# A diffusion step's expert lookup: more steps of the choice a chunk, and half of a product in three rounded parts

## The chip, the cores and the metric

One core of a Trainium2 chip runs the whole program. The metric is the time of one execution on the device in microseconds (us). Of the kernel before three runs are known: 5380.45, 5382.38 and 5386.86 us, median 5382.38.

## What is computed

One inference step of a backbone with two streams, 128 context tokens and 512 latent tokens of width 2048. The first half of the layer (a token mixer of three branches) isn't touched by the change. The second half, which is, looks up experts by product keys:

```python
v1, i1 = lax.top_k(s1, 16); v2, i2 = lax.top_k(s2, 16)     # 8 heads, 128 keys each
cand = (v1[..., :, None] + v2[..., None, :]).reshape(tok, 8, 256)
top, sel = lax.top_k(cand, 16)                             # 128 experts a token
g = jax.nn.softmax(top, axis=-1)
act = jnp.einsum("cd,ckd->ck", xc, u_tab[ic])              # first table, 16384 x 2048
w = gc * jax.nn.gelu(act)
out = jnp.einsum("ck,ckd->cd", w, v_tab[ic])               # second table, 16384 x 2048
```

Both tables are float32.

## The kernel before, in words

The 640 tokens are five blocks of 128. For each block `choose` (L1034) finds the experts that any token of the block uses: it writes a dense matrix of weights `G_d` (16384 experts by 128 tokens, mostly zeros) to memory in four stores of 2 MB from the tile `Gs`, and a list `L_d` of the used experts. `experts` (L1371) then goes over that list in chunks of 256 rows: it gathers 256 rows of the first table, multiplies them with the block's tokens, weighs the result, and adds the product with 256 rows of the second table to an accumulator in PSUM. The first 24 chunks of a block (K0) always run; each later one stands in an `If` on the length of the list. In this run there are 134 chunks in all.

One chunk is a generator, `chunk` (L1262), with nine yields. In the order of the program:

- `gather_u`: an indirect DMA, issued by POOL, for 128 rows of the first table into `ur` for the next chunk.
- `turn(g)` for g = 0 to 7 (L1229): four transposes of 128 columns into PSUM (`tb`), a copy to a rounded float32 half `wh` on ACT (L1237), the rest `wl` by a subtract on VectorE (DVE, L1238).
- `up(g)` (L1240): six products of 256 columns, three for each of two slices: rounded x rounded, rounded x rest, rest x rounded. A product of two rounded operands is one pass of TensorE; one of full float32 operands is two instructions of two passes each.
- the last `up` of a chunk, `up(7)`, stands in the next chunk and ends with the gelu on ACT (L1247). Then `weigh` (L1249) transposes the result and multiplies it with the weights `gr` on VectorE into `w`.
- `gather_g` (two gathers from `G_d` into `gr`), `entries` (two gathers of list entries `ix` for three chunks on), the second `gather_u`. All are issued by POOL.
- `down(u)` for u = 0 to 7 (L1256): one full float32 product of 512 columns each, of the half j = u // 4 of the weights with a quarter of `vr[j]`, the tile of 128 rows of the second table. In the steps g = 2 to 7 it stands between `turn(g)` and `up(g - 1)`; the last two stand at the end. These are the products of the chunk before.
- `gather_v(0)` refills `vr[0]` behind `down(3)`, `gather_v(1)` refills `vr[1]` at the chunk's end.

Each engine works off its instructions in this order. `pin` (L1357) ties every instruction of an engine to the one before it, so nothing is moved. POOL issues all the indirect gathers, one after the other.

The choice for the next block is itself a generator, advanced between the yields of the chunks: `more` takes a step at every odd yield of the first 24 chunks of a block (four a chunk), `fin`, the finishing of the last block, at every even one. What is left of the choice behind chunk 23 runs without a chunk beside it (`for _ in more: pass`). Its steps: 33 up to the one-hot tiles, then a loop of 34 rounds at L1102 in which VectorE writes one-hot tiles `oh` and `dd`, TensorE multiplies them (L1116), ACT copies the result to `Gs` (L1107), and after every eight results `Gs` is stored; four steps behind each store count the used experts (L1132); then 14 steps that write the list and gather its first entries. `Gs` is one buffer, so the next copy into it waits for the store.

Of the kernel before, what the change touches and what calls it, by code (L numbers as in the profile page):

```python
# [7 lines left out]
F32 = mybir.dt.float32  # L8
F32R = mybir.dt.float32r
# [142 lines left out]
class Kern:  # L152
# [881 lines left out]
    def choose(self, b, S=None):  # L1034
# [50 lines left out]
        g = I12[:, 2].rearrange("p (h k) -> p h k", k=16)  # L1085
# [10 lines left out]
        p = ps.tile([128, 3, 128], F32, name="g", tag="m", bufs=1)  # L1096
# [5 lines left out]
        for n in range(34):  # L1102
            if full is not None:
                n1, p = full
# [7 lines left out]
            if ready is not None:  # L1112
                n1, oh, dd = ready
                p = ps.tile([128, 4, 128], F32, name="g", tag="m", bufs=1)
# [4 lines left out]
            if n < 32:  # L1119
                oh = T.tile([128, 4, 128], F32, name="oh", tag="oa", bufs=2)  # L1120
                dd = T.tile([128, 4, 128], F32, name="dd", tag="od", bufs=2)
                for j in range(4):
                    k1, k2, w = (it[:, i, n * 4 + j:n * 4 + j + 1] for i in range(3))
# [6 lines left out]
            if n % 8 == 1 and n > 1:  # L1130
                for q in range(4):
                    v.tensor_reduce(cnt[:, n // 8 - 1, q * 32:q * 32 + 32], st[:, q * 32:q * 32 + 32], axis=AX.X,  # L1132
                                    op=ALU.add)
                    yield

        f = T.tile([128, 128], F32, name="f", tag="f", bufs=1)
        v.tensor_reduce(f, cnt.rearrange("p q i -> p i q"), axis=AX.X, op=ALU.add)
        v.tensor_scalar(f, f, 0.0, None, op0=ALU.is_gt)
# [6 lines left out]
        for r in range(16):  # L1145
            s = slice(r * 8, r * 8 + 8)
# [26 lines left out]
        p = ps.tile([128, 128], F32, name="g", tag="m", bufs=1)  # L1173
# [4 lines left out]
        p = ps.tile([128, 128], F32, name="g", tag="m", bufs=1)  # L1178
# [4 lines left out]
        p = ps.tile([128, 128], F32, name="g", tag="m", bufs=1)  # L1183
# [56 lines left out]
    def up(self, g, x):  # L1240
# [5 lines left out]
        if g == 7:  # L1246
            self.nc.scalar.activation(self.t, self.a, AF.Gelu_apprx_tanh)  # L1247

    def weigh(self):  # L1249

        p = self.bank()[:, :256].rearrange("p (j t) -> p j t", j=2)
        for j in range(2):
            self.nc.tensor.transpose(p[:, j], self.t[:, j * 128:j * 128 + 128], self.ident)  # L1253
        self.nc.vector.tensor_mul(self.w, p, self.gr)  # L1254

    def down(self, u, first):  # L1256

        j, d = divmod(u, 4)
        self.nc.tensor.matmul(self.acc[:, d], self.w[:, j], self.vr[j][:, d * 512:d * 512 + 512],  # L1259
                              start=first and j == 0, stop=j == 1, skip_group_check=True)  # L1260

    def chunk(self, i, c, pending, rows=None):  # L1262


        nc, b = self.nc, self.order[i]
        self.nbank = 1
        x = self.xs[i % 2]
        rows = rows or self.ur[c % 2]
        if c + 1 < NCH:
            self.gather_u(b, c + 1, 0)  # L1270
        self.turn(0, rows)
        if pending is not None:
            first, before = pending
            self.up(7, before)
        self.turn(1, rows)
        yield
        if pending is not None:
            self.weigh()
        self.gather_g(b, c)
        if c + 3 < NCH:  # L1280
            self.entries(b, c + 3)
        self.up(0, x)
        yield
        if c + 1 < NCH:
            self.gather_u(b, c + 1, 1)
        for g in range(2, 8):
            self.turn(g, rows)
            if pending is not None:
                self.down(g - 2, first)
                if g - 2 == 3:  # L1290
                    self.gather_v(b, c, 0)
            self.up(g - 1, x)
            yield
        if pending is not None:
            self.down(6, first)
            self.down(7, first)
        else:
            self.gather_v(b, c, 0)
        self.gather_v(b, c, 1)
        yield  # L1300
# [70 lines left out]
    def experts(self):  # L1371
        nc, tc = self.nc, self.tc
        E = self.E = self.pool("experts")
        one = lambda shape, name, dt=F32: E.tile(shape, dt, name=name)
        self.vr = [one([128, D], "vr%d" % j) for j in range(2)]
        self.y = one([128, D], "fy")
        self.t = one([128, CH], "t")
        self.gr, self.w = one([128, 2, 128], "gr"), one([128, 2, 128], "w")
        self.ur = [[one([128, D], "ur%d%d" % (c, j)) for j in range(2)] for c in range(2)]
        hb = self.H[GB]  # L1380
        self.xs = [[t[:, j] for t in hb] for j in range(2)]
        first = [one([128, D], "uf%d" % j) for j in range(2)]
        pieces = [[t[:, k * 512:k * 512 + 512]
                   for t in [self.wp.tile([128, 1024], F32R, name=n, tag=n, bufs=self.hl_bufs) for _ in range(3)]
                   for k in range(2)] for n in ("wh", "wl")]
        self.uh, self.ul = ([t.rearrange("p (k e) -> p k e", k=2) for t in p[:4]] for p in pieces)
        self.rr, self.nrow = [t.bitcast(F32) for p in pieces for t in p[4:]], 0
        self.fx = [self.wp.tile([128, 1024], F32, name="wr", tag="wr", bufs=self.raw_bufs) for _ in range(2)]
        ps = self.pool("ps5", space=PSUM)
        self.acc = ps.tile([128, 4, 512], F32, name="acc")  # L1390
        self.tb = [ps.tile([128, 512], F32, name="tb%d" % j) for j in range(2)]
        self.a = ps.tile([128, CH], F32, name="a")
        pending, rows, fin = None, None, iter(())
        mark = self.pin()
        self.load_x(0)
        for j in range(2):
            self.gather_u(self.order[0], 0, j)
        for i, b in enumerate(self.order):
            more = self.choose(self.order[i + 1]) if i < 4 else iter(())
            for c in range(K0):  # L1400
                if c == 0 and i:
                    fin = self.finish(i - 1)
                    next(fin)
                for n, _ in enumerate(self.chunk(i, c, pending, rows)):
                    next(more if n % 2 else fin if c else iter(()), None)
                if c == 0:
                    next(fin, None)
                rows, pending = None, (c == 0, self.xs[i % 2])
                if c == 0 and i < 4:
                    self.load_x(i + 1)  # L1410
            for _ in more:
                pass
            if i < 4:
                rows = first
                for j in range(2):
                    self.gather_u(self.order[i + 1], 0, j, first[j])
            n = nc.values_load(self.lists[b]["count"][0:1, 2:3].bitcast(I32), min_val=0, max_val=NE,
                               skip_runtime_bounds_check_because="it counts the ones among 16384 flags")
            self.pin(mark)
            pending = False, self.xs[i % 2]  # L1420
            with contextlib.ExitStack() as st:
                for c in range(K0, NCH):
                    st.enter_context(tc.If(n > c * CH, name="more%d_%d" % (i, c)))
                    mark = self.pin()
                    for _ in self.chunk(i, c, pending):
                        pass
                    self.pin(mark)
            mark = self.pin()
        self.nbank = 1
        self.up(7, pending[1])  # L1430
        self.weigh()
        for u in range(8):
            self.down(u, False)
        for _ in self.finish(4):
            pass
        self.pin(mark)
        self.close(ps, E)
# [95 lines left out]
```

## Time and profile before

| what | value |
|---|---|
| median of three runs | 5382.38 us |
| profiled execution | 5390.09 us |
| its span, first to last instruction | 5388.3 us |
| mean granted TensorE clock | 0.950 |
| TensorE busy (PE) | 4825.3 us, 90% |
| VectorE busy (DVE) | 2880.9 us, 53% |
| ScalarE busy (ACT) | 1604.0 us, 30% |
| GpSimd busy (POOL) | 1604.3 us, 30% |

The profile names engines PE, PEld (TensorE's weight loads, which overlap PE), DVE, ACT, POOL and SP. Matmuls are pipelined, so the time of one includes the way through the array; how long each really occupies the engine is the distance between two starts. The issuing of a DMA isn't counted as busy, except POOL's indirect ones. L12 is line 12 of the kernel.

### The profile page before, as it was taken

To read this page: it belongs to the slowest core of one execution; us is meant where nothing else is said; L and a number is where in the kernel's file an instruction comes from. 1 tells how busy PE (TensorE), PEld (TensorE's weight loads), DVE (VectorE), ACT (ScalarE), POOL (GpSimd) and SP (SyncE) were. 2 spreads that over 40 slices of the span, in tenths; PEclk is the share of its full clock that TensorE was granted. 3 is DMA by queue.
4 is the path that set the end of the run, shared out by engine and by line. 5 is a ranking of instruction groups with operands and counts; after the bars stand their busy time and mean duration, and the time that the engine had idled before them with its cause. 6 is when DMAs were issued, how large, how long until landed. Compare 5 with 4: busy or idle time off the path is not lost.

```text
span 5388.3 us, 74433 instructions
## 1 busy us (share of the span) xinstructions
PE 4825.3 (90%) x29015; PEld 4006.4 (74%) x29015; DVE 2880.9 (53%) x6240; ACT 1604.0 (30%) x2561; POOL 1604.3 (30%) x1628
## 2 busy tenths in 40 slices
PE   8999889999999979968999689877998699969997
PEld 3799879999999958758677567655776567746775
DVE  6783683566435553860754475456554564444333
ACT  3324324333132224232233123222332132212222
POOL 2000592000000016434443234323443343324443
PEclk9999999999999989989999799989998899979999
DMA  6544346555234466544677576756776677757665
GB/s 241 195 170 143 123 144 214 182 174 173 94 129 150 142 215 216 139 160 159 241 251 237 171 266 242 245 176 230 262 252 220 205 257 233 238 168 275 256 256 211
DMA packets 576710, 1084.99 MB, mean 201 GB/s; under 512 B 375643, under 2 KB 388955, under 8 KB 501819
## 3 DMA queue, kind: packets, MB, share of 16 engines
q0 software_dynamic: 97712, 596.41, 30.4%
q1 hardware_dynamic: 460394, 429.32, 27.0%
q10 hardware_dynamic: 18208, 54.08, 2.6%
q8 instruction: 239, 3.92, 0.3%
q14 instruction: 157, 1.28, 0.1%
HBM read 967.53 MB, written 112.13 MB: 200 GB/s over the span
## 4 chain that ended last, share of the span: by engine, by line
PE 29%; DMA 9%; DVE 6%; issue 5%; POOL 3%; ACT 2%; another core or an unknown queue 0%; POOLq 0%; DVEq 0%; SPq 0%; ACTq 0%
PE acc L1259 12%; PE a L1245 8%; DMA G_d<-Gs 6%; PE tb L1236 6%; PE g L1116 3%; DVE wl L1238 2%; ACT wh L1237 1%; DMA ix<-L_d,si 1%; POOL ix L1201 1%; POOL gr L1201 1%; PE tb L1253 1%; POOL ur L1201 1%; ACT Gs L1107 1%; DMA ur<-in_pu,ix 0%; DVE f L1149 0%
## 5 line engine op out<-in xcount | busy, mean ns | idle before, releaser
L1238 DVE TENSOR_TENSOR wl<-tb,wh 128x512 fp32r<-128x512 f32 x1072 | 737.6, 690 | 1387.8 <-ACT wh L1237 965.2
L1237 ACT CAST wh<-tb 128x512 fp32r<-128x512 f32 x1072 | 627.1, 586 | 1763.2 <-PE tb L1236 1517.8
L1259 PE MATMUL acc<-vr,w 128*128 128x512 f32 x2144 | 1094.3, 603 | 22.9 <-DVE w L1254 21.3
L1245 PE MATMUL a<-wh,hh 128*128 128x256 f32 x2144 | 957.6, 447 | 25.2 <-issue 18.3
L1236 PE MATMUL tb<-cst,ur 128*128 128x128 f32 x4160 | 645.2, 278 | 32.1 <-DMA ur<-in_pu,ix 30.9
L193 ACT CAST wh<-wr 128x1024 fp32r<-128x1024 f32 x339 | 355.6, 1049 | 977.4 <-PE a L630 364.6
L1245 PE MATMUL a<-wl,hh 128*128 128x256 f32 x2144 | 614.0, 286 | 20.5 <-DVE wl L1238 17.1
L1245 PE MATMUL a<-wh,hl 128*128 128x256 f32 x2144 | 609.8, 284 | 0.0
L1245 PEld LDWEIGHTS a<-wh,hh 128*128 128x128 f32 x2144 | 414.9, 193 | 229.5 <-issue 218.2
L1236 PEld LDWEIGHTS tb<-cst,ur 128*128 128x128 f32 x4160 | 491.5, 143 | 121.7 <-issue 83.2
L1245 PEld LDWEIGHTS a<-wl,hh 128*128 128x128 f32 x2144 | 415.6, 194 | 221.4 <-issue 168.2
L1201 POOL DMA_INDIRECT vr<-in_pv,ix x268 | 253.8, 947 | 1066.7 <-PE acc L1259 1037.2
L630 PE MATMUL a<-h,wl 128*128 128x320 f32 x2368 | 548.4, 311 | 18.4 <-DVE wl L194 18.4
L194 DVE TENSOR_TENSOR wl<-wr,wh 128x1024 fp32r<-128x1024 f32 x281 | 343.8, 1225 | 379.5 <-ACT wh L193 368.0
L630 PE MATMUL a<-h,wh 128*128 128x320 f32 x2368 | 546.7, 311 | 0.0
L630 PE MATMUL a<-l,wh 128*128 128x320 f32 x2368 | 543.7, 310 | 0.0
L630 PEld LDWEIGHTS a<-h,wl 128*128 128x128 f32 x2368 | 398.9, 189 | 20.7 <-DVE wl L194 20.0
L630 PEld LDWEIGHTS a<-h,wh 128*128 128x128 f32 x2368 | 403.4, 189 | 12.1
L1245 PEld LDWEIGHTS a<-wh,hl 128*128 128x128 f32 x2144 | 412.4, 192 | 0.0
L1259 PEld LDWEIGHTS acc<-vr,w 128*128 128x128 f32 x2144 | 341.4, 194 | 94.5 <-issue 68.8
L630 PEld LDWEIGHTS a<-l,wh 128*128 128x128 f32 x2368 | 398.7, 189 | 0.8
L1201 POOL DMA_INDIRECT ix<-L_d,si x298 | 290.3, 974 | 308.0 <-DVE si L1189 212.0
(396 smaller groups left out, 7489.0 us busy)
## 6 DMA issues: line engine op xcount, KB each, us to landing
wr<-in_wmod SPq DMA_DIRECT2D x152, 512.0 KB
wr<-in_win SPq DMA_DIRECT2D x83, 512.0 KB
G_d<-Gs SPq DMA_DIRECT2D x20, 2048.0 KB
wrx<-in_win SPq DMA_DIRECT2D x69, 512.0 KB
wrx<-in_wmod SPq DMA_DIRECT2D x40, 512.0 KB
wr<-in_wo SPq DMA_DIRECT2D x36, 512.0 KB
wr<-in_wq SPq DMA_DIRECT2D x32, 512.0 KB
wrx<-in_wq SPq DMA_DIRECT2D x32, 512.0 KB
```

Source lines behind the costliest of these rows:

```text
L193: nc.scalar.copy(h, raw)
L194: (eng or nc.vector).tensor_sub(l, raw, h.bitcast(F32))
L630: nc.tensor.matmul(a, w, x[:, kt, c0:c0 + n], start=kt == 0 and i == 0, stop=kt == nk - 1 and i == 2)
L1107: nc.scalar.copy(st[:, :, n1 % 8 * 4:n1 % 8 * 4 + 4], p.rearrange("j t i -> j i t"))
L1116: nc.tensor.matmul(p[:, j], oh[:, j], dd[:, j], start=True, stop=True)
L1201: self.nc.gpsimd.indirect_dma_start(out=out, out_offset=None, in_=table, in_offset=bass.IndirectOffsetOnAxis(ap=idx, axis=0))
L1236: nc.tensor.transpose(p[:, k, j * 128:j * 128 + 128], rows[j][:, kt * 128:(kt + 1) * 128], self.ident)
L1237: nc.scalar.copy(self.uh[g % 4], p)
L1238: nc.vector.tensor_sub(self.ul[g % 4], p, self.uh[g % 4].bitcast(F32))
L1245: self.nc.tensor.matmul(self.a, a[:, kt], w[:, k], start=kt + n == 0, stop=kt == 15 and n == 2)
L1253: self.nc.tensor.transpose(p[:, j], self.t[:, j * 128:j * 128 + 128], self.ident)
L1259: self.nc.tensor.matmul(self.acc[:, d], self.w[:, j], self.vr[j][:, d * 512:d * 512 + 512], start=first and j == 0, stop=j == 1, skip_grou ...
```

## The change

The choice advances at every yield, nine steps a chunk, and twenty steps that do nothing follow the four counting steps behind each of the first three stores. `fin` takes the odd yields. The half `vr[0]` of the second table's rows is split by quarters: ACT copies a quarter to a rounded tile `vh`, POOL subtracts it from the row to give the rest `vl`. The weights' first half is split too (`Wh` on ACT, `Wl` on VectorE). `down` takes three products of rounded operands for that half, and the full product for the other. `gather_v(0)` moves from behind `down(3)` to before `down(2)`. `vh` and `vl` lie in a part of older tiles that is free then.

```diff
+                for _ in range(20 if n < 32 else 0):
+                    yield
...
+    def split_v(self, d):
+
+        s = slice(d * 512, d * 512 + 512)
+        self.nc.scalar.copy(self.vh[:, s], self.vr[0][:, s])
+        self.nc.gpsimd.tensor_sub(self.vl[:, s], self.vr[0][:, s], self.vh[:, s].bitcast(F32))
...
         self.nc.vector.tensor_mul(self.w, p, self.gr)
+        self.nc.scalar.copy(self.Wh, self.w[:, 0])
+        self.nc.vector.tensor_sub(self.Wl, self.w[:, 0], self.Wh.bitcast(F32))
...
         j, d = divmod(u, 4)
-        self.nc.tensor.matmul(self.acc[:, d], self.w[:, j], self.vr[j][:, d * 512:d * 512 + 512],
-                              start=first and j == 0, stop=j == 1, skip_group_check=True)
+        s = slice(d * 512, d * 512 + 512)
+        for n, (w, x) in enumerate(((self.w[:, 1], self.vr[1][:, s]),) if j else
+                                   ((self.Wh, self.vh[:, s]), (self.Wh, self.vl[:, s]), (self.Wl, self.vh[:, s]))):
+            self.nc.tensor.matmul(self.acc[:, d], w, x, start=first and j == n == 0, stop=j == 1,
+                                  skip_group_check=True)
...
             first, before = pending
+            self.split_v(0)
             self.up(7, before)
         self.turn(1, rows)
+        if pending is not None:
+            self.split_v(1)
         yield
...
             self.turn(g, rows)
             if pending is not None:
+                if g < 4:
+                    self.split_v(g)
+                if g == 4:
+                    self.gather_v(b, c, 0)
                 self.down(g - 2, first)
-                if g - 2 == 3:
-                    self.gather_v(b, c, 0)
             self.up(g - 1, x)
...
                 for n, _ in enumerate(self.chunk(i, c, pending, rows)):
-                    next(more if n % 2 else fin if c else iter(()), None)
+                    next(more, None)
+                    if c and n % 2:
+                        next(fin, None)
```

Behind the last chunk of all, four `split_v` stand ahead of `weigh`.

## Rows read from the trace of the kernel before

**Rows 1.** The page: busy time by engine, and one of the costliest groups.

```profile
PE 4825.3 (90%) x29015; PEld 4006.4 (74%) x29015; DVE 2880.9 (53%) x6240; ACT 1604.0 (30%) x2561; POOL 1604.3 (30%) x1628
...
L1116 PE MATMUL g<-dd,oh 128*128 128x128 f32 x1280 | 208.5, 313 | 108.5 <-ACT Gs L1107 99.8 <-DVE dd L1125 8.6
```

**Rows 2.** Line 1247, the gelu: duration in ns; whole run, then 2970 to 3210.

```profile
L1247 ACT ACTIVATE t<-a x134: 383/383/384, 2582.7 to 5351.4; 128x256 f32<-128x256 f32 x134
...
L1247 ACT ACTIVATE t<-a x9: 383/383/384, 2975.5 to 3204.7; 128x256 f32<-128x256 f32 x9
```

**Rows 3.** Windows, one chunk: length, busy us (instructions) of PE, PEld, DVE, ACT, POOL; clock.

```profile
5143.68:5160.69 17.01, 16.66 (x100) 12.39 (x98) 5.86 (x9) 5.07 (x9) 7.61 (x8) 1.00 0.70 258
```

**Rows 4.** Timeline of TensorE in that chunk: start, us, instructions merged.

```profile
5150.95 0.60 PE L1236 MATMUL tb<-cst,ur 128*128 128x128 f32 x4
5151.38 1.02 PE L1259 MATMUL acc<-vr,w 128*128 128x512 f32 x2
5151.84 0.69 PE L1245 MATMUL a<-wh,hh 128*128 128x256 f32 x1
...
5152.96 0.60 PE L1236 MATMUL tb<-cst,ur 128*128 128x128 f32 x4
...
5158.98 1.88 PE L1259 MATMUL acc<-vr,w 128*128 128x512 f32 x4
```

**Rows 5.** Timeline of POOL in that chunk; in brackets the idle time before.

```profile
5144.12 0.94 POOL L1201 DMA_INDIRECT vr<-in_pv,ix  x1 [5.38 <-PE acc L1259]
...
5148.69 0.96 POOL L1201 DMA_INDIRECT gr<-G_d,ix  x1 [0.30 <-issue]
5149.95 0.95 POOL L1201 DMA_INDIRECT ix<-L_d,si  x1 [0.30 <-issue]
...
5154.84 0.95 POOL L1201 DMA_INDIRECT vr<-in_pv,ix  x1 [1.42 <-PE acc L1259]
5161.12 0.94 POOL L1201 DMA_INDIRECT vr<-in_pv,ix  x1 [5.34 <-PE acc L1259]
```

**Rows 6.** Waits of POOL over the run: us in total, times, longest.

```profile
POOL vr L1201 <- PE acc L1259: 1037.2, 246, 11.6
```

**Rows 7.** The chain that ended last, at the first block's end: start, us, what.

```profile
2990.12 30.22 DMA G_d<-Gs
...
3040.31 4.61 DVE cnt L1132 x4
...
3064.01 0.95 POOL ix L1201
```

**Rows 8.** Timeline of TensorE in an earlier stage: products of rounded operands, 512 columns.

```profile
1900.51 0.39 PE L957 MATMUL a<-wh,hh 128*128 128x512 f32 x1
1900.74 0.40 PE L957 MATMUL a<-wl,hh 128*128 128x512 f32 x1
```

**Rows 9.** Line 301 on POOL: least, median and most ns of one.

```profile
L301 POOL TENSOR_TENSOR x<-x,xp x16: 1265/1293/2284, 1904.9 to 2163.2; 128x512 f32<-128x512 f32 x16
```

**Rows 10.** Windows around stops of TensorE; the sum is over seven stretches behind stops.

```profile
2917.82:2923.11 5.29, 0.01 (x1) 0.01 (x1) 0.72 (x4) 0.58 (x1) 1.95 (x2) 0.71 0.93 326
2923.11:2926.88 3.77, 3.77 (x15) 3.25 (x15) 0.19 (x1) 0.58 (x1) 0.00 (x0) 0.50 0.26 104
...
3497.74:3503.73 5.99, 5.99 (x22) 4.96 (x23) 0.69 (x1) 0.58 (x1) 0.00 (x0) 0.50 0.02 8
...
sum 30.49, PE 30.48 PEld 26.02 DVE 7.09 ACT 3.58 POOL 2.68; mean PE 4.35 PEld 3.72 DVE 1.01 ACT 0.51 POOL 0.38
```

**Rows 11.** Timelines of POOL and VectorE side by side, in two earlier stretches.

```profile
1989.93 2.41 POOL L194 TENSOR_TENSOR wl<-wr,wh 128x1024 fp32r<-128x1024 f32 x1 [42.76 <-ACT wh L193]
...
1990.20 0.69 DVE L965 TENSOR_TENSOR gy<-a,r 128x512 f32<-128x512 f32 x1 [1.91 <-PE a L957]
...
2163.18 2.27 POOL L301 TENSOR_TENSOR x<-x,xp 128x512 f32<-128x512 f32 x1
...
2158.64 5.66 DVE L1076 TENSOR_TENSOR oh<-oa,cst 128x1024 f32<-128x1024 f32 x2
```

More of the change, by code (lines that the diff above doesn't have):

```diff
@@ L1381, in experts @@
         self.xs = [[t[:, j] for t in hb] for j in range(2)]
+        self.vh, self.vl = (t[:, 2].rearrange("p k t -> p (k t)") for t in hb)
+        self.Wh, self.Wl = (one([128, 128], n, F32R) for n in ("Wh", "Wl"))
         first = [one([128, D], "uf%d" % j) for j in range(2)]
@@ L1430, in experts @@
         self.up(7, pending[1])
+        for d in range(4):
+            self.split_v(d)
         self.weigh()
```

## The prediction, made before the changed kernel ran

> **What bounds the kernel now.** I read the page first: TensorE is busy 90% of the span and no other engine over 53% [rows 1]. An average hides stages, so I asked next for the gelu at L1247, which runs once a chunk: 134 of them, from 2582.7 to 5351.4 us [rows 2]. The 133 intervals between them are 2769 us, half of the span, and everything that the diff touches lies in them. The windows view of one late chunk, 5143.68 to 5160.69, shows 17.01 us with TensorE busy 16.66, ACT 5.07, DVE 5.86 and POOL 7.61 [rows 3]: there TensorE is the bound. The timeline of TensorE gives the parts of one step of g, 2.01 us from 5150.95 to 5152.96: four transposes 0.43, one `down` 0.86 (two passes of 0.43; the first `up` is issued behind the first pass), six `up` products 0.12 each, so 0.70 [rows 4]. The last two `down` take 1.71 [rows 4].
>
> Then the timeline of POOL, which issues eight gathers a chunk [rows 5]. Consecutive ones start 1.25 us apart: 0.95 and a gap of 0.30. What the reader is to see is the wait at the head: the gather into `vr[1]` may not start before the last `down` of the chunk before has read that tile, so POOL stands 5.34 us and starts at 5161.12, 0.43 us behind the chunk's boundary. All of POOL's work for a chunk comes after this point. In total POOL waits 1037.2 us in 246 waits for L1259 [rows 6]. Today that costs nothing, since nothing in the same chunk waits for what POOL issues.
>
> Four times a block ends differently. From 2975.5 to 3204.7 there are nine gelus, so eight intervals in 229 us where 8 x 17.0 = 136 would do: 93 us too long [rows 2]. The chain of waits shows why: the rest of the choice is drained with no chunk beside it. It waits 30.22 us for a store of `Gs`, goes on to the counts at 3040.31 and reaches the first gather of entries at 3064.01 [rows 7].
>
> **The change part by part.** The numbers are in the time of the profiled execution (5390.09 us, span 5388.3); the median of the runs is 5382.38, 7.7 lower.
>
> *Choice in nine steps.* The choice has 129 steps. At four a chunk, 24 chunks take 96; 33 are drained. With 60 empty ones it has 189, and nine a chunk end it in 21 chunks. The drain from 2990.12 to 3064.01 takes 74 us; a chunk's 17 and some 7 for products of L1116 in it have to be done anyway, so about 50 us goes from each of four block ends, some 200 us. 24 steps (four counts, 20 empty) follow a store before its buffer is written again, 2.7 chunks or more than 45 us, longer than the 30.22 us store, so the waits at L1107 for it go too; these are short, since the products of L1116 wait 99.8 us in all [rows 1]. TensorE's work in the choice is unchanged.
>
> *Three rounded products.* A 512-column product of rounded operands starts 0.23 us after the one before [rows 8]; three take 0.70 where the full product takes 0.86. Four a chunk save 0.64 us, 86 us over 134 chunks.
>
> *The splits.* On ACT four copies and a small one add some 2.6 us at 0.59 each (5.07 less the gelu's 0.38 [rows 2], over eight) to 5.07: ACT has the room. Each also gets a subtract on POOL. The nearest row is the 128x512 add of L301, 1.29 us in the median [rows 9]; I take 1.29, with 1.27 and 2.28, its least and its most, as ends. POOL's sum is 8 x 1.25 + 4 x 1.29 = 15.2 us, under a chunk, and by busy time it would be hidden. By order it is not. POOL's queue in a chunk becomes: `vr[1]` (waits for the last `down`), `ur`, split 0, split 1, `gr`, `gr`, `ix`, `ix`, `ur`, split 2, split 3, `vr[0]`. Counted from the boundary E: 0.43 to the start of the first gather, two gathers and their gaps 2.5, two subtracts 2.6, five gathers and gaps 6.2, the third subtract 1.3: 13.0, and some 0.4 for two more gaps before and behind subtracts and the signal to TensorE, which no row shows for this pair (0 to 0.7). So `vl`'s third part is ready at **E + 13.4**.
>
> TensorE asks for it in `down` 2, at 5151.38 today, E + 7.7 [rows 4], and about 0.3 later behind the longer start of the chunk. It stands about 5.4 us. After that come two of the three products 0.47, `up` 0.70, the step of g = 5 at 1.83, two steps of 2.01 and the last two `down` 1.71: 8.7 us to the next boundary. Split 3 is ready at E + 14.7, before its `down` at some E + 15. The `vr[0]` gather starts at E + 15, half a chunk before the copy that needs it, and needs no term. The ring POOL, `down` 2, `down` 7, POOL is 13.4 + 8.7 = **22.1 us** a chunk where there were 17.0.
>
> *The clock.* TensorE never stood so long in a steady chunk. Elsewhere it did: in 2917.82 to 2923.11 it was idle for 5.29 us, its granted clock fell, and it was 0.50 for the next 3.77 us [rows 10]. 0.50 is the lower of its two levels, 1.2 GHz. Seven stretches behind idle times of 3.9 to 6.4 us that I looked at ran 30.49 us at 0.50, 4.36 each [rows 10], so 2.2 us of work lost each time. The changed chunk has such a stop in every round, ahead of `down` 2: **24.3 us**. The bounds are 0 (the gap is filled by the choice's products) and 3 us (the longest of the seven).
>
> *What is left at block ends.* Of the 93 us, some 43 are not the drain. I keep 20 of them, since the longer ring hides part (0 to 43). The six entry gathers of the next block now stand in POOL's ring instead of the drain: 7.5 us. The choice's TensorE work is 208.5 us over five blocks by its busy time [rows 1], 42 each; what falls ahead of `down` 2 is free, the rest, 13 us, is not (0 to 42). Together 40 a block, 160 in all.
>
> *Sum.* 133 x 24.3 + 160 = 3392 us, where 2769 stood: 623 more. 5390 + 623 = 6013, less 7.7 is 6005; I say **6000 us**.
>
> *A rule against the row.* POOL's subtract is priced by the add of L301 [rows 9]. The Trainium skill, GPSIMD Engine Reference, "Performance versus the Vector engine", gives 4497 ns for a two-input fp32 operation over 2048 elements, 1.96 times VectorE's, and advises VectorE for such work; a quarter of it would be an estimate of 1.12 us, the ring 0.5 us shorter and the total some 68 us lower. The row has its own fixed part and stands.
>
> **The rivals.**
>
> *Faster: POOL keeps up.* If the third subtract were done when TensorE asks, the chunk would save 0.64 us and the drain would go: 86 + 200 + some 45 of store waits = 331, 5050 us. What decides is the time from the boundary to that subtract: at 8 us it is hidden, and the total breaks even at a ring of (2769 - 160) / 133 = 19.6 us, that is at some 9 us with the clock's loss or 11 without. For it speaks only POOL's sum of 15.2 us; against it that five gathers stand between split 1 and split 2 at 1.25 each [rows 5]. Chance 0.09.
>
> *The clock holds.* The steady chunks have TensorE busy three quarters of the time, and the choice fills some stops. Then the ring is 22.1, 133 x 22.1 + 160 = 3099, 330 more: 5710 us. Against it stand the seven stretches. Chance 0.20.
>
> *VectorE holds POOL up.* Beside an L1076 of two SBUF inputs, the L301 add took 2.27 us instead of 1.29; beside L965, which reads one input from PSUM, a subtract kept its 2.41 [rows 11]. The split's neighbour is L1238, which reads PSUM as L965 does, so I expect no loss. If it counts, three subtracts cost 1.0 more each: ring 27.2, 133 x 27.2 + 160 = 3778, 1009 more, 6390 us. The Trainium skill, Advanced Engine Details and Errata, "Mode Summary", says that VectorE's second SBUF port is shared with GPSIMD and that two-port instructions and GPSIMD block each other; whether L1238 is one of them the page doesn't say. Chance 0.06.
>
> My forecast has the other 0.65.
>
> **The numbers.** 6000 is the likeliest case. Its low end without any gap around the subtracts and without the clock is a ring of 21.5, with extras of 120: some 5600. Its high end is a ring of 26 with extras of 180, some 6260. The range 5600 to 6260 takes in "the clock holds" and leaves out the two outer rivals. Runs of this kernel lie within 0.12% of each other; 0.2%, 11 us, is what can be told from no change. Faster 0.10, within 0.2% 0.02, slower 0.88.
>
> **What would show it.** The gelus would be some 24 us apart (22 with a full clock). TensorE would wait for POOL's subtract ahead of the second product of `down` 2, some 5 us a chunk, and for nothing else as long; the granted clock would be 0.50 behind that. POOL would run without a break from `vr[1]` to `vr[0]` and then wait 7 to 9 us for the last `down`. At block ends no wait of 30 us for `Gs` would be left. If gelus stand under 19.6 us apart the prediction's sign is wrong; if POOL shows idle time ahead of split 2, or the subtract takes 2 us, its mechanism is.

## The result, and the profile after

The changed kernel takes 5985.09 us (median of four runs, 5981.37 to 5991.95) where the kernel before took 5381.41 beside it: a ratio of 1.1122, with a 95% interval of 1.1103 to 1.1142. It is slower by 604 us. The forecast was 6000.

First the page of the changed kernel: its busy time by engine, and its chain of waits by engine and by line. TensorE is busy 174 us longer, part of it at the lower clock (below), but in a longer span, so its share falls from 90 to 83% [rows 1]. POOL's share of the chain rises from 3 to 14%; its subtract is on it now (`hl` is the tile in which `vl` lies, `hh` that of `vh`). First the chain's shares before, then three lines of the page after:

```profile
PE 29%; DMA 9%; DVE 6%; issue 5%; POOL 3%; ACT 2%; another core or an unknown queue 0%; POOLq 0%; DVEq 0%; SPq 0%; ACTq 0%
```

```profile
PE 4998.9 (83%) x29551; PEld 4281.2 (71%) x29551; DVE 3127.9 (52%) x6374; ACT 1889.4 (32%) x3231; POOL 2272.6 (38%) x2164
...
PE 20%; POOL 14%; DVE 9%; issue 9%; DMA 3%; ACT 3%; POOLq 0%; ACTq 0%; DVEq 0%
PE acc L1273 9%; PE a L1248 6%; POOL ix L1204 4%; POOL gr L1204 4%; PE tb L1239 4%; POOL hl L1256 4%; POOL ur L1204 2%; DMA ix<-L_d,si 2%; DVE Wl L1265 2%; PE g L1116 1%; ACT hh L1255 1%; ACT wh L1240 1%; DVE wl L1241 1%; DVE oh L1124 1%; DMA ur<-in_pu,ix 1%
```

The gelu's line, first over the whole run, then from 3190 to 3325:

```profile
L1250 ACT ACTIVATE t<-a x134: 377/387/388, 2594.0 to 5954.7; 128x256 f32<-128x256 f32 x134
...
L1250 ACT ACTIVATE t<-a x5: 377/386/388, 3194.0 to 3321.6; 128x256 f32<-128x256 f32 x5
```

The 133 intervals are 3361 us instead of 2769 [rows 2]: 592 us more, nearly all of the slowdown. The median of the last undisturbed ones, worked out from their starts, is 23.9 us instead of 17.0. The second row is a block's start: four intervals in 127.6 us, 32 each, which the ring doesn't explain.

One late chunk, from the first `turn` to the next. The windows view (columns as in [rows 3]): the whole chunk, then TensorE's stop, then the stretch behind it.

```profile
5641.80:5665.71 23.91, 19.25 (x104) 15.21 (x102) 7.18 (x10) 7.23 (x14) 12.64 (x12) 0.86 0.52 182
...
5650.70:5654.48 3.78, 0.23 (x2) 0.01 (x1) 0.69 (x1) 0.58 (x1) 3.23 (x4) 0.79 0.27 75
5654.48:5658.50 4.02, 4.02 (x15) 3.63 (x16) 0.02 (x1) 0.59 (x1) 2.12 (x2) 0.50 0.77 269
```

POOL's timeline in that chunk:

```profile
5642.24 0.95 POOL L1204 DMA_INDIRECT vr<-in_pv,ix  x1 [9.27 <-PE acc L1273]
5643.49 0.95 POOL L1204 DMA_INDIRECT ur<-in_pu,ix  x1 [0.30 <-issue]
5644.46 2.52 POOL L1256 TENSOR_TENSOR hl<-vr,hh 128x512 fp32r<-128x512 f32 x2
5647.14 0.97 POOL L1204 DMA_INDIRECT gr<-G_d,ix  x1 [0.16 <-DVE Wl L1265]
...
5652.18 0.95 POOL L1204 DMA_INDIRECT ur<-in_pu,ix  x1 [0.30 <-issue]
5653.15 2.49 POOL L1256 TENSOR_TENSOR hl<-vr,hh 128x512 fp32r<-128x512 f32 x2
5655.92 0.96 POOL L1204 DMA_INDIRECT vr<-in_pv,ix  x1 [0.27 <-POOL hl L1256]
```

And TensorE's:

```profile
5641.80 0.60 PE L1239 MATMUL tb<-cst,ur 128*128 128x128 f32 x4
...
5647.19 0.50 PE L1273 MATMUL acc<-hh,Wl 128*128 128x512 f32 x1 [0.71 <-DVE Wl L1265]
...
5650.44 0.48 PE L1273 MATMUL acc<-hh,Wh 128*128 128x512 f32 x1
5654.48 0.79 PE L1273 MATMUL acc<-hl,Wh 128*128 128x512 f32 x1 [3.55 <-POOL hl L1256]
...
5663.99 1.88 PE L1273 MATMUL acc<-vr,w 128*128 128x512 f32 x4
```

Read them together. POOL waits 9.27 us for the last `down` (5.34 before, [rows 5]), then works with no gap over 0.30 us. The third subtract starts behind five gathers and ends some 1.25 us after 5653.15. TensorE has done the first product of `down` 2 and stands 3.55 us for it; the clock falls to 0.50; from 5654.48 to the boundary at 5665.71 it takes 11.23 us. Behind a few stops of the same length the clock didn't fall. Here is one: the clock behind it is 1.00, and from 5773.98 to the next boundary at 5782.84 TensorE takes 8.86 us.

```profile
5773.98 0.51 PE L1273 MATMUL acc<-hl,Wh 128*128 128x512 f32 x1 [3.56 <-POOL hl L1256]
...
5782.84 0.60 PE L1239 MATMUL tb<-cst,ur 128*128 128x128 f32 x4
```

```profile
5773.98:5778.00 4.02, 4.02 (x27) 3.55 (x28) 0.69 (x1) 0.83 (x2) 2.14 (x2) 1.00 0.77 273
```

Over the run TensorE waits for this line in two kinds of row, one for products and one for weight loads:

```profile
PE acc L1273 <- POOL hl L1256: 401.0, 126, 7.1
...
PEld acc L1273 <- POOL hl L1256: 440.5, 126, 7.4
```

### The profile page after: what moved, and what is told of

The parts are those of the page before. It is cut to its first block, busy times and chain, and to the rows that moved or that the text cites. A ratio compares the mean times of both kernels' runs of the same rounds, so it can differ in the third digit from the quotient of the medians.

```text
span 5990.2 us, 76800 instructions
## 1 busy us (share of the span) xinstructions
PE 4998.9 (83%) x29551; PEld 4281.2 (71%) x29551; DVE 3127.9 (52%) x6374; ACT 1889.4 (32%) x3231; POOL 2272.6 (38%) x2164
## 4 chain that ended last, share of the span: by engine, by line
PE 20%; POOL 14%; DVE 9%; issue 9%; DMA 3%; ACT 3%; POOLq 0%; ACTq 0%; DVEq 0%
PE acc L1273 9%; PE a L1248 6%; POOL ix L1204 4%; POOL gr L1204 4%; PE tb L1239 4%; POOL hl L1256 4%; POOL ur L1204 2%; DMA ix<-L_d,si 2%; DVE Wl L1265 2%; PE g L1116 1%; ACT hh L1255 1%; ACT wh L1240 1%; DVE wl L1241 1%; DVE oh L1124 1%; DMA ur<-in_pu,ix 1%
## 5 line engine op out<-in xcount | busy, mean ns | idle before, releaser
L1241 DVE TENSOR_TENSOR wl<-tb,wh 128x512 fp32r<-128x512 f32 x1072 | 736.9, 688 | 1806.8 <-ACT wh L1240 1805.8
L1248 PE MATMUL a<-wh,hh 128*128 128x256 f32 x2144 | 783.6, 365 | 3.9 <-issue 3.9
L1239 PE MATMUL tb<-cst,ur 128*128 128x128 f32 x4160 | 690.8, 293 | 42.4 <-DMA ur<-in_pu,ix 28.9
L1248 PE MATMUL a<-wl,hh 128*128 128x256 f32 x2144 | 653.2, 305 | 42.6 <-DVE wl L1241 42.4
L1256 POOL TENSOR_TENSOR hl<-vr,hh 128x512 fp32r<-128x512 f32 x536 | 673.8, 1280 | 35.5 <-ACT hh L1255 29.3
L1273 PE MATMUL acc<-hl,Wh 128*128 128x512 f32 x536 | 266.9, 498 | 401.0 <-POOL hl L1256 401.0
L1248 PEld LDWEIGHTS a<-wl,hh 128*128 128x128 f32 x2144 | 455.4, 212 | 148.7 <-DVE wl L1241 58.4
L1273 PE MATMUL acc<-vr,w 128*128 128x512 f32 x1072 | 529.3, 596 | 0.0
L1248 PEld LDWEIGHTS a<-wh,hh 128*128 128x128 f32 x2144 | 457.4, 213 | 98.9 <-issue 66.7
L1248 PEld LDWEIGHTS a<-wh,hl 128*128 128x128 f32 x2144 | 453.2, 211 | 0.0
L1273 PEld LDWEIGHTS acc<-hl,Wh 128*128 128x128 f32 x536 | 124.9, 233 | 440.8 <-POOL hl L1256 440.5
```

Source lines behind the costliest of these rows:

```text
L1239: nc.tensor.transpose(p[:, k, j * 128:j * 128 + 128], rows[j][:, kt * 128:(kt + 1) * 128], self.ident)
L1241: nc.vector.tensor_sub(self.ul[g % 4], p, self.uh[g % 4].bitcast(F32))
L1248: self.nc.tensor.matmul(self.a, a[:, kt], w[:, k], start=kt + n == 0, stop=kt == 15 and n == 2)
L1256: self.nc.gpsimd.tensor_sub(self.vl[:, s], self.vr[0][:, s], self.vh[:, s].bitcast(F32))
L1273: self.nc.tensor.matmul(self.acc[:, d], w, x, start=first and j == n == 0, stop=j == 1, skip_group_check=True)
```

## The experiments

**The choice alone.** The kernel before with the steps of the change:

```diff
-                    next(more if n % 2 else fin if c else iter(()), None)
+                    next(more, None)
+                    if c and n % 2:
+                        next(fin, None)
...
+                for _ in range(20 if n < 32 else 0):
+                    yield
```

> The choice in nine steps with its empty steps, and nothing of the split. Theory: the slowdown is not from here. The drains at four block ends go (200 us) and the waits behind stores (some 45), but the first 33 steps of a choice are nearly all VectorE's and now fall into four chunks: VectorE, 94% busy there in the changed kernel, bounds some 4 chunks a block, about 30 us a block more than before. Sum 5381 - 245 + 120 = 5260 us (5180 to 5340). Rival, the choice's new pace is what costs: over 5500 us.

Measured: 5274.29 us, ratio 0.9795 (0.9778 to 0.9811). The choice's new pace is a gain of 2%, and the slowdown isn't from it. Late chunks are 17.0 us as before. Six chunks at a block's start are longer: 31.5, 31.7, 24.2, 21.4, 20.7 and 21.3 us (intervals of the gelu).

**The split alone.** The changed kernel without those lines.

> The split and its three products, with the choice at four steps a chunk as before. Theory: the ring of POOL's queue is all here. The gelus stay some 24 us apart, the drain comes back and VectorE's bound at block starts goes: 5985 + 200 - 4 x 37 = 6040 us (5950 to 6130). Rival, the choice's new pace costs: under 5500 us.

Measured: 6033.77 us, ratio 1.1207 (1.1185 to 1.1230). Late chunks are 23.9 us as in the changed kernel. The drains are back, in four intervals of the gelu of 61 to 68 us (70 to 73 in the kernel before). With the run before it this settles which part costs. With the split in place the choice's pace gains 49 us (6033.77 less 5985.09), not 110.

**Two gathers moved.** The gathers of list entries go behind splits 2 and 3 on POOL's queue:

```diff
-        if c + 3 < NCH:
+        if pending is None and c + 3 < NCH:
             self.entries(b, c + 3)
...
                     self.split_v(g)
+                if g == 3 and c + 3 < NCH:
+                    self.entries(b, c + 3)
```

> The changed kernel with the two gathers of entries moved on POOL's queue from before to behind splits 2 and 3; nothing else. Theory: the third subtract is 2.5 us earlier, at 10.2 us behind the boundary; TensorE's stop shrinks from some 3.6 to 1 us and no longer takes the clock with it, so the ring is 10.2 + 8.7 = 18.9 us instead of 23.9. Total 5985 - 133 x 5.0 = 5320 us (5250 to 5450). If the clock falls all the same: 5985 - 133 x 2.5 = 5650 us. Rival, the place of two gathers does not matter: 5985 us.

Measured: 5581.80 us, ratio 1.0368 (1.0347 to 1.0389). A late chunk in the windows view, and TensorE's wait in the timeline:

```profile
5419.57:5438.61 19.04, 16.88 (x104) 13.11 (x102) 7.18 (x10) 7.24 (x14) 12.67 (x12) 1.00 0.67 229
```

```profile
5429.74 0.50 PE L1273 MATMUL acc<-hl,Wh 128*128 128x512 f32 x1 [1.05 <-POOL hl L1256]
```

For late chunks the expectation held to 0.2 us: two gathers of 1.26 us less ahead of the subtract took 4.9 us off the chunk, since behind the shorter stop the clock is still 1.00. The total is 260 us over the expected one: the chunks beside the choice are 18 to 27 us long, those at a block's start up to 33, and the ring had hidden part of that. A part of what holds them shows in the run of POOL's order with the weights in PSUM, below.

**The stop filled.** 28 products of 256 columns behind the first product of `down` 2, into the second half of the bank in which `a` lies (`fill_to`). The kernel's outputs change by some 7% with them, and no run settles how. The rest of the work and its order are as in the changed kernel, so the times can be compared.

```diff
+FILLS = 28
...
+            if u == 2 and n == 0:
+                for _ in range(FILLS):
+                    self.nc.tensor.matmul(self.fill_to, self.Wh, self.vh[:, :256], start=True, stop=True,
+                                          skip_group_check=True)
```

> The changed kernel with 28 products of 256 columns more in each chunk, placed into TensorE's stop ahead of the second product of down 2; they write to a part of PSUM that nothing reads. Theory: the stop costs twice, by its length and by the clock that falls behind it; with the stop filled the clock stays at full and the stretch from the third subtract to the boundary takes 8.8 us instead of 11.2. Late chunks 21.5 instead of 23.9 us, total 5985 - 133 x 2.0 to 2.4 = 5670 to 5720 us although 3752 products were added. Rival, the clock has no part in it: 5985 us, or more where the added products run over the stop (up to 6400).

Measured: 5903.50 us, ratio 1.0936 (1.0906 to 1.0965): 82 us less than the changed kernel with 3.52 us more of products in each chunk (101 us less when each is set against the kernel before beside it, 5400.67 us here). A late chunk, its added products and what follows:

```profile
5724.85:5746.41 21.56, 20.23 (x132) 16.51 (x131) 7.18 (x10) 7.24 (x14) 12.70 (x12) 1.00 0.59 202
```

```profile
5733.79 3.52 PE L1278 MATMUL a<-hh,Wh 128*128 128x256 f32 x28
5737.54 0.50 PE L1274 MATMUL acc<-hl,Wh 128*128 128x512 f32 x1 [0.24 <-POOL hl L1257]
```

The granted clock is 1.00 throughout and the late chunk 21.6 us, as expected to 0.1 us. From the subtract at 5737.54 to the boundary it takes 8.87 us, as behind the stop at 5773.98 above, with no product added: 2.3 us a chunk are the clock's. The total misses the expected range by 180 us. Beside the choice many of TensorE's waits for this subtract are under 3 us in the changed kernel (36 of 89 up to 5100 us), less than the added products take, so the chunks there gain little: many still take 25 to 29 us.

**POOL's order.** Splits 2 and 3 go right behind splits 0 and 1:

```diff
         if pending is not None:
             self.weigh()
+            self.split_v(2)
+            self.split_v(3)
+            if c + 1 < NCH:
+                self.gather_u(b, c + 1, 1)
+            self.gather_v(b, c, 0)
+        elif c + 1 < NCH:
+            self.gather_u(b, c + 1, 1)
         self.gather_g(b, c)
...
-        if c + 1 < NCH:
-            self.gather_u(b, c + 1, 1)
...
-                if g < 4:
-                    self.split_v(g)
-                if g == 4:
-                    self.gather_v(b, c, 0)
```

> All of the change and all of POOL's work, in another order on its queue: splits 2 and 3 right behind 0 and 1, then the second gather for the next chunk, the refill of vr[0], and only then the four gathers of weights and entries. Theory: order alone costs, so the third subtract is ready some 7 us behind the boundary, before TensorE asks for it at 8.9; the ring opens, TensorE binds again at 16.5 to 17.5 us a chunk, its clock stays at full. Total 5100 to 5300 us, 5200 likeliest. Rival, it is the amount of POOL's work (12.6 us busy a chunk, 15.2 with gaps) or the subtracts' time: over 5700 us.

Measured: 5742.95 us, ratio 1.0665 (1.0648 to 1.0683). The expectation failed: late chunks are 21.7 and 22.7 us by turns. The subtracts came when they were wanted, but another wait took their place. POOL and VectorE in a late chunk, and TensorE's wait:

```profile
5578.58 4.94 POOL L1256 TENSOR_TENSOR hl<-vr,hh 128x512 fp32r<-128x512 f32 x4
```

```profile
5579.84 3.84 DVE L1265 TENSOR_TENSOR Wl<-w,Wh 128x128 fp32r<-128x128 f32 x1 [0.36 <-ACT Wh L1264]
5583.60 0.68 DVE L1241 TENSOR_TENSOR wl<-tb,wh 128x512 fp32r<-128x512 f32 x1
```

```profile
5583.73 0.79 PE L1273 MATMUL acc<-hh,Wl 128*128 128x512 f32 x1 [3.14 <-DVE Wl L1265]
```

The subtract for `Wl`, 128 elements wide, takes 3.84 us; it ends when POOL's run of four has ended, and L1241 behind it has to wait. Its least time in this run is 0.29. It reads two operands from SBUF. L1241, which reads one from PSUM, takes 0.67 to 0.69 us throughout the run, beside POOL's subtracts or not.

**The same with the weights in PSUM.** To test that reading, `w`'s first half goes to PSUM:

```diff
-        self.nc.vector.tensor_mul(self.w, p, self.gr)
-        self.nc.scalar.copy(self.Wh, self.w[:, 0])
-        self.nc.vector.tensor_sub(self.Wl, self.w[:, 0], self.Wh.bitcast(F32))
+        self.nc.vector.tensor_mul(p[:, 0], p[:, 0], self.gr[:, 0])
+        self.nc.vector.tensor_mul(self.w[:, 1], p[:, 1], self.gr[:, 1])
+        self.nc.scalar.copy(self.Wh, p[:, 0])
+        self.nc.vector.tensor_sub(self.Wl, p[:, 0], self.Wh.bitcast(F32))
```

> As the run with the splits in front on POOL's queue (5743 us), but the first half of the weights is written to PSUM, so that VectorE's subtract for Wl reads one input from PSUM and one from SBUF. Theory: in that run Wl took 3.84 us instead of 0.29 because an instruction of VectorE with two SBUF inputs stands while POOL's four subtracts run one behind the other; from PSUM it takes 0.3, TensorE's stop of 3.1 us ahead of down 0 goes and the clock with it. Late chunks 16.5 to 17.5 us instead of 22.2, total 5250 to 5450 us (in the chunks beside the choice VectorE still meets POOL). Rival, VectorE is held by any work of POOL whatever it reads: 5700 to 5750 us.

Measured: 5503.85 us, ratio 1.0198 (1.0172 to 1.0224). VectorE and POOL in a late chunk, and the windows of two late chunks:

```profile
5308.29 0.29 DVE L1266 TENSOR_TENSOR Wl<-tb,Wh 128x128 fp32r<-128x128 f32 x1 [0.33 <-ACT Wh L1265]
5309.82 0.69 DVE L1241 TENSOR_TENSOR wl<-tb,wh 128x512 fp32r<-128x512 f32 x1 [1.24 <-ACT wh L1240]
```

```profile
5306.86 5.02 POOL L1256 TENSOR_TENSOR hl<-vr,hh 128x512 fp32r<-128x512 f32 x4
```

```profile
5252.39:5269.80 17.41, 16.57 (x103) 13.10 (x103) 6.32 (x11) 7.11 (x14) 12.62 (x12) 1.00 0.69 250
5304.20:5321.12 16.92, 16.36 (x104) 13.19 (x103) 6.32 (x11) 7.11 (x14) 12.64 (x12) 1.00 0.76 250
```

0.29 us in the middle of POOL's 5.02. So this instruction isn't held up by POOL's work as such: it is held with two SBUF inputs, and not with one of them in PSUM. The ring is open and the clock full, and most late chunks take 17.4 us: more than the 17.0 without the split. In these TensorE waits once more, at the chunk's start, for `wl` of the last `turn`; in four of the last 25 it doesn't, and they take 16.9. What delays that `wl` the profile doesn't name.

```profile
5269.80 0.66 PE L1239 MATMUL tb<-cst,ur 128*128 128x128 f32 x4 [0.27 <-DVE wl L1241]
```

The total is 54 us over the expected range's top; in the chunks beside the choice VectorE still meets POOL. From 2600 to 3250 us the one-hot instruction of L1124 takes 0.28 to 0.29 us in the mean where POOL has no subtracts (the choice alone, and the run below with the subtracts on VectorE), and 0.41 to 0.46 where it has them (this run, and the one with two gathers moved). In that order, from the four traces:

```profile
L1124 DVE TENSOR_SCALAR oh<-cst,itT 128x128 f32<-128x128 f32 x168 | 48.5, 289 | 1.7 <-ACT itT L1099 1.7
...
L1124 DVE TENSOR_SCALAR oh<-cst,itT 128x128 f32<-128x128 f32 x128 | 36.3, 284 | 0.4 <-ACT itT L1099 0.4
...
L1124 DVE TENSOR_SCALAR oh<-cst,itT 128x128 f32<-128x128 f32 x128 | 52.9, 413 | 2.1 <-ACT itT L1099 2.1
...
L1124 DVE TENSOR_SCALAR oh<-cst,itT 128x128 f32<-128x128 f32 x128 | 58.5, 457 | 1.0 <-ACT itT L1099 1.0
```

One of them in this run, with the subtract that had begun just before it; it ends with that subtract, and the next takes 0.28 us:

```profile
2666.75 1.26 POOL L1256 TENSOR_TENSOR hl<-vr,hh 128x512 fp32r<-128x512 f32 x1 [1.43 <-ACT hh L1255]
...
2666.80 1.30 DVE L1124 TENSOR_SCALAR oh<-cst,itT 128x128 f32<-128x128 f32 x1
...
2668.27 0.28 DVE L1124 TENSOR_SCALAR oh<-cst,itT 128x128 f32<-128x128 f32 x1
```

It reads one tile in SBUF and writes one there, so two SBUF inputs aren't the only case. Nor is every instruction that works in SBUF alone lengthened: the reduction of L1132 takes 1.21 us in all four traces.

**Only the weights in PSUM**, in the changed kernel with its own order (the same four lines).

> The changed kernel with the weights' first half in PSUM and nothing else. Theory: Wl falls from 1.41 us to 0.3 and the 0.71 us that TensorE waits for it ahead of the third product of down 0 goes, but that lies ahead of the stop at down 2, which takes it up: the ring stays at 23.9 to 24.2 us, total 5985 us within 30. Rival, the wait for Wl is a part of the ring: 5985 - 133 x 0.7 = 5890 us.

Measured: 6009.50 us, ratio 1.1132 (1.1096 to 1.1168): no gain over the changed kernel's 1.1122, and late chunks of 23.9 us. The wait of 0.71 us for `Wl` in the changed kernel lies ahead of the stop and is taken up by it.

**The subtracts on VectorE.** One word, `gpsimd` to `vector`, in `split_v`.

> The changed kernel with its four subtracts of a chunk on VectorE instead of POOL. Theory: what costs is that the third subtract stands behind five gathers on POOL's queue; on VectorE it is ready a few us behind the boundary, and POOL has its eight gathers as before. TensorE binds again in late chunks (16.5 to 17.5 us, clock at full); in the chunks beside the choice VectorE has 2.7 us a chunk more and binds more of them, 19 to 23 us. Total 5200 to 5400 us, 5300 likeliest. Rival, the copies on ACT and the longer chain of the weights' halves cost: late chunks over 19 us, total over 5500.

Measured: 5549.44 us, ratio 1.0280 (1.0246 to 1.0314); late chunks 18.2 us, where 16.5 to 17.5 had been expected. The total is in the rival's range, the late chunks lie between the two. The ring is open, but TensorE now waits elsewhere. Two rows of TensorE, and one of ACT:

```profile
5345.80 0.44 PE L1262 MATMUL tb<-cst,t 128*128 128x128 f32 x2 [1.95 <-ACT t L1250]
5348.26 0.51 PE L1273 MATMUL acc<-hh,Wh 128*128 128x512 f32 x1 [0.61 <-ACT Wh L1264]
```

```profile
5344.85 0.62 ACT L1255 CAST hh<-vr 128x512 fp32r<-128x512 f32 x1 [1.52 <-DMA vr<-in_pv,ix]
```

The copies stand ahead of the gelu and of `Wh` on ACT, in a stretch where TensorE has nothing else to do, and the first copy itself waits 1.52 us for the gather into `vr[0]` to land. With VectorE's added work two chunks at a block's start take 34 to 36 us, where the choice alone has 32.

**The choice paced.** The choice alone again, but in the first seven chunks of a block at four steps:

```diff
-                    next(more, None)
+                    if c > 6 or n % 2:
+                        next(more, None)
...
-                for _ in range(20 if n < 32 else 0):
+                for _ in range(16 if n < 32 else 0):
```

> The choice alone, without the split, paced: four steps a chunk in the first seven chunks of a block, where its steps are VectorE's, nine in the other 17, and 16 empty steps behind a store. In the run of the choice alone six chunks at each block's start took 142 us where six of 17.0 would take 102; before they took 110 to 125. Theory: that excess is VectorE's and goes with the pace, so 4 x 20 to 40 us less than 5274: 5165 us (5100 to 5210), faster than both kernels. Rival, the excess belongs to the block's change (branches, the finishing of the last block) and stays: 5274 us.

Measured: 5241.78 us, ratio 0.9728 (0.9712 to 0.9745), the fastest kernel of the study and 743 us under the changed one. It gained 33 us, a third of the expected 109: the second block's first chunks fell from 31.5 and 31.7 to 22.1 and 25.5 us, but the loop's steps now begin at full pace in chunk 7 and lengthen chunks there to 22 to 24 us. VectorE's work is the same; a pace spreads it and doesn't remove it.

**The same pace with the open split.**

> The same pace in the run with the splits in front on POOL's queue and the weights' first half in PSUM (5504 us). It says whether the split is worth anything once its wait is gone. Theory: late chunks stay at 17.4 us against 17.0 without the split, and beside the choice POOL's subtracts and VectorE's work still hold each other up, so it loses to the choice alone: 5504 less the same 80 to 160 us, 5380 us (5330 to 5430). Rival, the three products pay once the choice is paced: under the paced choice alone, 5150 us or less.

Measured: 5435.05 us, ratio 1.0087 (1.0069 to 1.0105), 5 us over the expected range: 193 us more than the same pace without a split. Late chunks are 17.4 against 17.0. In this form three rounded products for one don't pay here even without the wait for the subtract.

## Why the prediction was right, point by point

**The ring.** The reading held: what decides is the order on POOL's queue and the wait at its head, not POOL's busy share (12.64 us of 23.91). The third subtract was ready at E + 12.7 instead of 13.4 (5654.48 less 5641.80): a subtract starts 0.02 us behind a gather (5644.46 after 5643.49 + 0.95), where I had put a gap. The subtract's 1.29 us was 1.25 to 1.28. Moving two gathers and filling the stop both gave the ring that the sum gives, 19.0 and 21.6 us.

**The stop and the clock.** TensorE stood 3.55 us, not 5.4, as the subtract was ready 0.7 us earlier and it came to `down` 2 some 1.1 us later: the chain of `w`, `Wh`, `Wl` had been priced with no wait of its own, and `Wl` cost 0.71. That moved nothing, as the run with the weights in PSUM shows. The stretch behind the subtract took 11.23 us where 8.7 + 2.2 had been summed. The clock's part is 2.3 us by the filled stop, 2.2 in the prediction. Ring 23.9 against 24.3. That the total came within 15 us is partly luck: the ring's 0.4 us are 53 us over the run, and other terms made up for them.

**What is left at block ends.** 3361 - 133 x 23.9 is 182 us against 160, but the term is right in size only, and that was luck. I had put it together from left-overs, entries and the choice's products. The runs show two other things. The first interval of 32 us at a block's start is a late landing: ACT's first copy waits 8.63 us for the gather into `vr[0]`, and TensorE 9.11 us for the gelu behind it. It does so at all four block ends, 5.4 to 9.0 us each, 31 us in all, where the prediction says that this gather "needs no term". Why it lands so late there wasn't tried. The others are VectorE's: 33 steps that are nearly all its own fall into four chunks. Two intervals of 32 us stand there in the run of the choice alone too, and pacing takes them down to 22 to 26. The copy that waits, and two windows of the changed kernel: VectorE is busy 9.17 of 30.00 us around that copy, then 31.03 of 33.00.

```profile
3226.07 0.62 ACT L1255 CAST hh<-vr 128x512 fp32r<-128x512 f32 x1 [8.63 <-DMA vr<-in_pv,ix]
```

```profile
3205.00:3235.00 30.00, 17.48 (x82) 13.95 (x83) 9.17 (x34) 5.54 (x11) 8.46 (x8) 0.74 0.58 209
3235.00:3268.00 33.00, 20.09 (x94) 14.72 (x94) 31.03 (x119) 5.97 (x12) 10.74 (x10) 0.81 0.45 145
```

In the prediction neither was priced. The drains did go, but the choice alone gained 110 us and not the 245 that I had for drains and store waits.

**The rivals.** "POOL keeps up" was rightly unlikely, and its price of 5050 us was wrong: with the wait gone the kernel takes 5504, as the split's longer way to the first `down` eats most of the 0.64 us and VectorE and POOL meet beside the choice. Before, the first `down` starts 3.70 us behind the boundary at 5143.68; in the run with the weights in PSUM it starts 4.11 behind the one at 5304.20:

```profile
5147.38 1.02 PE L1259 MATMUL acc<-vr,w 128*128 128x512 f32 x2
```

```profile
5308.31 0.50 PE L1274 MATMUL acc<-hh,Wh 128*128 128x512 f32 x1 [0.17 <-ACT Wh L1265]
```

"The clock holds" fell with the trace: 0.50 behind most stops of 3.3 us and more, and at full only in single chunks, as at 5773.98. "VectorE holds POOL up" didn't happen: L1256 takes 1.26 to 1.33 us throughout (up to 2.28 in the two runs with the splits in front). It was the other way about, and I had not thought of that way. The rule that I cited for it (the Trainium skill, Advanced Engine Details and Errata, "Mode Summary") says that GPSIMD instructions and two-port instructions of VectorE block each other, and names no direction. The prediction has it that the page leaves open whether L1238 is one of them; but its table asks of them that source and destination lie in SBUF, and L1238 reads PSUM. The 1.30 us of the one-hot instruction fit it; whether it counts `Wl`, with its two inputs and 3.84 us, as two-port that section doesn't say.

**The rule on POOL's pace** (the Trainium skill, GPSIMD Engine Reference, "Performance versus the Vector engine") gave an estimate of 1.12 us a subtract; the trace has 1.28.

**A sum.** The range's low end was added up wrongly: a ring of 22.1 without the 0.4 of gaps is 21.7, not 21.5, and the low end 5620, not 5600. Nothing hangs on it.

## What to carry to other kernels

An engine with idle time can't take on work for free when its queue is in order: find what stands at its head, count from the event that frees the head to the place of the new work, and compare with when the result is asked for. POOL was busy for half of a chunk, and yet the ring through it made each round 7 us longer, of which more than 2 were the clock that fell behind the stop. When a generator's steps are made denser, look at whose work the densest ones are: here it was VectorE's, and of the 245 us that I had put on drains and store waits the choice alone gained 110.

## What the runs showed that was not expected

A subtract of VectorE with two SBUF inputs can stand while POOL's subtracts run one behind the other, until the last of them ends: 3.84 us for one of 0.29, and everything behind it on VectorE waits too. Moving one of its two inputs to PSUM took 4.8 us off a chunk (the same order of POOL: 21.7 and 22.7 us by turns in SBUF, 17.4 in PSUM). The one-hot instructions, with one SBUF input and an SBUF output, were lengthened as well (0.29 to 0.46 us in the mean), and not where the subtracts were VectorE's own (0.28). Which other instructions this hits wasn't tried. And work added in a stop made a kernel faster: 28 products a chunk, 82 us less.
